# Elementwise work of a token mixer taken off GpSimd and given to VectorE and ScalarE

## The chip, the cores and the metric

The kernel runs on one core of a Trainium2 chip. The metric is device microseconds from the start to the end of one execution; lower is better. A core has five engines that each run their own instructions in a fixed order and wait for one another by semaphores: TensorE (PE in the profile; its weight loads are the row PEld), VectorE (DVE), ScalarE (ACT), GpSimd (POOL) and SyncE (SP), which here only issues DMA transfers.

## The reference

One decoder layer on 1024 tokens of width 1024, all in float32: a half-step feed-forward network (FFN) with layer norm, a token mixer with layer norm, a second half-step FFN with layer norm, and a gated embedding. The change touches the mixer alone. Cut to what it touches:

```
z = x1 @ w_in                                   # 1024 x 1024 -> 3872 columns
# four retention pairs of heads (u), chunks of 128 tokens
q, k = rotary(q), rotary(k) / 8                 # t*cos + swapped(t)*sin
ret  = (q k^T * decay) v + (q * qdecay) @ state
ret_out = silu(g) * (groupnorm(ret) * gain + bias)
# four RWKV-7 pairs of heads (u): one step for each token
state = state * w_t - (state @ kk_t) b_t + v_t k_t ;  y_t = state @ r_t
k  = k * (1 + (a - 1) * k_a)
rw_out  = (groupnorm(y) * gain + bias + bonus * v) * gate
x2 = layer_norm(alpha * x1 + [ret_out, rw_out] @ w_out)
```

The token-by-token recurrence is computed in chunks of 128 tokens. The log decays are summed along a chunk (`cs`), and each chunk's factors are `exp(cs - middle)` and `exp(middle - cs)`, where the middle is `cs` at token 64 of the chunk.

## The kernel before

The mixer takes about 700 to 1550 us of the span. Features lie on the 128 partitions and tokens along the free axis. The RWKV part has 8 units: four head pairs `u`, each with two halves `h` of 512 tokens, so names such as `w2_1` or `r1_1` are unit `u_h` of RWKV (w) or of retention (r). The loop over steps `s` in `mixer` does, at step `s`, for three units at different stages: `rw_operands` of unit `s+1` (products with the chunk factors, and a triangular inverse by 31 pairs of small VectorE instructions, `itw` L1040 and `ixw` L1042, in `substitution`), `doublings` and `rw_chunks` of unit `s` (the chain over the four chunks through the state `wst`), `rw_inputs` of unit `s+2` (shift, low-rank projections, decays, normalised keys), and `retention` of unit `s`.

The products `z` with the weights `w_in` are filler for TensorE: 28 tiles (`z_tile`) at a low priority, 48 products of 128x512 each. As float32 is split into a high and a low part (`split`: ScalarE casts the high part, L47; another engine subtracts it to make the low part, L48), each product is three matmuls, L61 to L63, and L63 needs the low part `lo_win`. The split of a tile's weights can't begin before the matmuls on the tile before have read the same buffers. When the z tiles are done, the products with `w_out` (`wopo`, weights and rows split into `mw`) are the filler.

Nobody writes an order by hand: a list scheduler orders each engine's instructions at build time, by dependencies, the priorities in the code, and its own estimates of durations. On the chip the order is fixed, so an instruction that waits holds up all that stand behind it on its engine.

GpSimd does in the mixer, before the change: the low parts of `w_in` (54 of 56 instructions) and half of those for `w_out`; in `rw_inputs` the subtraction of the middle (`ccw` L953), two small instructions for the state's factor `few`, and the product of the keys `wkw` L982; in `rw_operands` `arw` L1013 and `kpw` L1015; in `rw_chunks` the scaled state `sfw` L1136 and two products of the output, `wow` L1155 and L1156; in `retention` four rotary instructions (L842, L844), the decay of q (`zqr` L867) and the output's product (`ror` L902). The bonus product on TensorE, `bnpw` L987, needs `rkw` L985 on VectorE, which needs `wkw` L982 on GpSimd, which comes after `kkw` L981 on VectorE. The transpose `ktpr` needs `zkr` L844.

## Time and profile before

| | us |
|---|---|
| median of 3 runs | 2352.06 (2345.69 to 2354.2) |
| profiled execution | 2348.16 |
| its span in the profile | 2346.4 |
| TensorE busy | 2247.1 (96%) |
| VectorE busy | 1631.9 (70%) |
| ScalarE busy | 833.8 (36%) |
| GpSimd busy | 755.3 (32%) |

The profile is one execution. 1.8 us of its time lie outside the span. Busy time of an engine counts its instructions from start to end; on TensorE matmuls overlap and their ends are modelled, so the times between starts say more than the busy share. The granted clock is that of TensorE, as a share of 2.4 GHz.

### The profile page before, as it was taken

The page shows a single profiled execution, that of the slowest core. Times are in us where ns is not written, and L with a number is a line of the kernel's source. Part 1 is how long each engine was busy: PE and PEld are TensorE (multiplying, and loading weights), DVE is VectorE, ACT ScalarE, POOL GpSimd, SP SyncE. Part 2 cuts the span into 40 slices and gives each one's busy share as a digit, 9 for nine tenths or more (in the row PEclk, how much of TensorE's full clock was granted, in tenths as well). Part 3 has the DMA queues.
Part 4 walks back from the last instruction along what each step waited for, and adds up shares of the span by engine and source line. Part 5 has one row for each costly group of instructions (what it writes and reads, how often), then busy time and mean ns, then how long its engine had stood idle before and what let it go on. Part 6 is the DMA issues. An engine that isn't in the chain of part 4 may idle for free.

```text
span 2346.4 us, 31303 instructions
## 1 busy us (share of the span) xinstructions
PE 2247.1 (96%) x11009; PEld 1801.9 (77%) x11009; DVE 1631.9 (70%) x2643; ACT 833.8 (36%) x1418; POOL 755.3 (32%) x614
## 2 busy tenths in 40 slices
PE   7999999999999999999999999998999999999999
PEld 5888888788786667777677777766888888788787
DVE  7776867765782378576774777689676767966862
ACT  4322232344652523232332323263323232445550
POOL 4346464300102323334433433225555553000220
PEclk9999999999999999799999999999999999999999
DMA  4345555497335443133333363323464644974321
GB/s 145 122 152 177 173 190 166 162 334 237 89 121 180 145 130 96 58 117 113 96 102 118 94 187 116 99 90 104 153 195 155 202 144 148 354 256 149 111 77 41
DMA packets 288963, 345.97 MB, mean 147 GB/s; under 512 B 35715, under 2 KB 162150, under 8 KB 288806
## 3 DMA queue, kind: packets, MB, share of 16 engines
q1 hardware_dynamic: 284224, 331.34, 44.2%
q0 software_dynamic: 3328, 12.06, 1.3%
q8 instruction: 87, 1.43, 0.3%
q10 hardware_dynamic: 1254, 0.58, 0.1%
q14 instruction: 70, 0.57, 0.1%
HBM read 237.47 MB, written 106.43 MB: 147 GB/s over the span
## 4 chain that ended last, share of the span: by engine, by line
PE 77%; DVE 14%; issue 3%; DMA 3%; POOL 2%; ACT 1%; SPq 0%; ACTq 0%; DVEq 0%; POOLq 0%
PE f2m L62 5%; PE f2m L63 5%; PE f2m L61 5%; PE f1m L61 5%; PE f1m L62 5%; PE f1m L63 5%; PE z L63 3%; PE z L61 3%; PE z L62 3%; DVE ixw L1042 2%; DVE itw L1040 2%; PE scpw L1102 2%; PE f1qa L61 1%; PE f1qa L62 1%; PE f1qa L63 1%
## 5 line engine op out<-in xcount | busy, mean ns | idle before, releaser
L61 PE MATMUL z<-x1Th,hi_win 128*128 128x512 f32 x448 | 188.2, 420 | 4.6 <-ACT hi_win L47 4.6
L63 PE MATMUL z<-x1Th,lo_win 128*128 128x512 f32 x448 | 188.2, 420 | 4.5 <-POOL lo_win L48 3.4
L62 PE MATMUL z<-x1Tl,hi_win 128*128 128x512 f32 x448 | 187.9, 419 | 0.0
L1040 DVE TENSOR_TENSOR itw<-iltw,ixw 32x31 f32<-32x31 f32 (+15 forms) x248 | 114.1, 460 | 24.3 <-DMA iltw<-scrw 10.7
L1042 DVE TENSOR_TENSOR ixw<-ixw,itw 32x31 f32<-32x31 f32 (+15 forms) x248 | 110.4, 445 | 4.5
L48 POOL TENSOR_TENSOR lo_win<-raw_win,hi_win 128x512 fp32r<-128x512 f32 x54 | 75.9, 1407 | 116.5 <-ACT hi_win L47 102.3
L61 PEld LDWEIGHTS z<-x1Th,hi_win 128*128 128x128 f32 x448 | 86.9, 194 | 28.5 <-ACT hi_win L47 5.7
L63 PEld LDWEIGHTS z<-x1Th,lo_win 128*128 128x128 f32 x448 | 86.4, 193 | 26.7 <-POOL lo_win L48 5.8
L62 PEld LDWEIGHTS z<-x1Tl,hi_win 128*128 128x128 f32 x448 | 86.4, 193 | 19.9 <-issue 2.1
L149 POOL TENSOR_TENSOR f2tb<-f2tb,f2tb 128x512 f32<-128x512 f32 x44 | 71.5, 1626 | 80.4 <-DMA f2tb<-in_ffn_w_down 74.4
L149 POOL TENSOR_TENSOR f1tb<-f1tb,f1tb 128x512 f32<-128x512 f32 x44 | 69.7, 1583 | 70.4 <-DMA f1tb<-in_ffn_w_down 66.1
L48 DVE TENSOR_TENSOR f1hl<-f1s,f1hh 128x512 fp32r<-128x512 f32 x63 | 45.5, 723 | 62.4 <-ACT f1hh L47 62.4
L48 DVE TENSOR_TENSOR f2hl<-f2s,f2hh 128x512 fp32r<-128x512 f32 x63 | 44.9, 713 | 44.4 <-ACT f2hh L47 44.4
L47 ACT CAST f1hh<-f1s 128x512 fp32r<-128x512 f32 x63 | 39.2, 622 | 92.2 <-PE f1qa L62 38.6
L47 ACT CAST f2hh<-f2s 128x512 fp32r<-128x512 f32 x63 | 39.2, 622 | 89.7 <-PE f2qb L62 35.1
L1136 POOL TENSOR_SCALAR sfw<-wst,few 64x64 f32<-64x64 f32 x48 | 30.1, 628 | 125.8 <-DVE wst L1137 77.0
L1110 DVE COPY_PREDICATED scz<-mask,scpw 128x384 f32<-128x384 uint8 x64 | 36.7, 584 | 46.6 <-PE scpw L1105 38.8
L108 DVE TENSOR_TENSOR f2S<-f2w 128x512 f32<-128x512 f32 x22 | 20.6, 939 | 65.2 <-DMA f2w<-in_ffn_w_gu 62.4
L62 PE MATMUL f2qa<-f2vl,f2hh 128*128 128x512 f32 x164 | 64.1, 391 | 0.7 <-DVE f2vl L48 0.7
L63 PE MATMUL f2qa<-f2vh,f2hl 128*128 128x512 f32 x164 | 64.0, 390 | 0.3 <-DVE f2hl L48 0.3
L62 PE MATMUL f1qa<-f1vl,f1hh 128*128 128x512 f32 x164 | 63.9, 389 | 0.0
L63 PE MATMUL f1qa<-f1vh,f1hl 128*128 128x512 f32 x164 | 63.8, 389 | 0.0
(786 smaller groups left out, 7117.5 us busy)
## 6 DMA issues: line engine op xcount, KB each, us to landing
f1w<-in_ffn_w_gu SPq DMA_DIRECT2D x44, 512.0 KB
f2w<-in_ffn_w_gu SPq DMA_DIRECT2D x44, 512.0 KB
f1s<-hd SPq DMA_DIRECT2D x63, 256.0 KB
f2s<-hd SPq DMA_DIRECT2D x63, 256.0 KB
zs<-zs SPq DMA_DIRECT2D x56, 256.0 KB
raw_win<-in_w_in SPq DMA_DIRECT2D x54, 256.0 KB
f1tb<-in_ffn_w_down SPq DMA_DIRECT2D x44, 256.0 KB
wt<-f1tb SPq DMA_DIRECT2D x44, 256.0 KB
```

The source lines that it names most:

```text
L47: self.last_split = self.nc.scalar.copy(hi, src).ins
L48: (eng or self.nc.vector).tensor_tensor(out=lo, in0=src, in1=hi, op=ALU.subtract)
L61: mm(ps, a[0], b[0], start=first, stop=False)
L62: mm(ps, a[0], b[1], start=False, stop=False)
L63: mm(ps, a[1], b[0], start=False, stop=last)
L108: sub = lambda o, a, b, op=ALU.subtract: V.tensor_tensor(out=o, in0=a, in1=b, op=op)
L149: nc.gpsimd.tensor_tensor(out=t, in0=a, in1=b, op=ALU.subtract)
L1040: nc.vector.tensor_tensor(out=t, in0=lt[:, j, j + 1:].unsqueeze(2).broadcast_to([B, n, c]), in1=x[:, j:j + 1, 0:c].broadcast_to([B, n, c]) ...
L1042: nc.vector.tensor_tensor(out=x[:, j + 1:, 0:c], in0=x[:, j + 1:, 0:c], in1=t, op=ALU.add)
L1102: nc.tensor.matmul(ps[e][:, 0:2 * P], kp[rr, cs], ar[rr, c].rearrange("p a t -> p (a t)"), start=True, stop=True)
L1110: nc.vector.copy_predicated(z, self.mask, ps[e][:, 0:3 * P].rearrange("p (a t) -> p a t", a=3))
L1136: nc.gpsimd.tensor_scalar(out=sf[rr], in0=st[rr, rr], scalar1=fe[rr, c:c + 1], scalar2=None, op0=ALU.mult)
```

## The change

All arithmetic that GpSimd did in the mixer goes to VectorE, but for the scaled state `sfw`, which goes to ScalarE. GpSimd keeps its memsets and DMA issues. The subtraction of the middle is dropped: ScalarE's exponentials take the middle as a bias for each partition instead, so that each chunk needs its own two instructions (8 for a unit where there were 2), and VectorE makes the four negated middles (`mid`). The output of an RWKV unit, before one ScalarE and two GpSimd instructions, becomes two VectorE instructions with a scalar for each partition.

```diff
# retention (both q and k)
-            nc.gpsimd.tensor_tensor(out=b, in0=b, in1=sin, op=ALU.mult)
+            nc.vector.tensor_tensor(out=b, in0=b, in1=sin, op=ALU.mult)
             nc.vector.tensor_tensor(out=a, in0=a, in1=cos, op=ALU.mult)
-            nc.gpsimd.tensor_tensor(out=a, in0=a, in1=b, op=ALU.add)
+            nc.vector.tensor_tensor(out=a, in0=a, in1=b, op=ALU.add)
-        nc.gpsimd.tensor_tensor(out=qd, in0=qd, in1=qdec.broadcast_to([P, 4, P]), op=ALU.mult)
+        nc.vector.tensor_tensor(out=qd, in0=qd, in1=qdec.broadcast_to([P, 4, P]), op=ALU.mult)
-        nc.gpsimd.tensor_tensor(out=t, in0=t, in1=th, op=ALU.mult)
+        nc.vector.tensor_tensor(out=t, in0=t, in1=th, op=ALU.mult)
# rw_inputs
-        cc = tmp("cc", 4 * (P + 1)).rearrange("p (c t) -> p c t", c=4)
-        nc.gpsimd.tensor_tensor(out=cc, in0=cs, in1=cs[:, :, 64:65].broadcast_to([P, 4, P + 1]), op=ALU.subtract)
+        mid = T("mid", [4])
+        nc.vector.tensor_scalar(out=mid, in0=cs[:, :, 64], scalar1=-1.0, scalar2=None, op0=ALU.mult)
-        nc.scalar.activation(w.eP, cc, AF.Exp)
-        nc.scalar.activation(w.eM, cc[:, :, 1:], AF.Exp, scale=-1.0)
+        for c in range(4):
+            nc.scalar.activation(w.eP[:, c], cs[:, c], AF.Exp, bias=mid[:, c:c + 1])
+            nc.scalar.activation(w.eM[:, c], cs[:, c, 1:], AF.Exp, bias=cs[:, c, 64:65], scale=-1.0)
-        nc.gpsimd.tensor_copy(w.fe, w.eP[:, :, P])
-        nc.gpsimd.tensor_tensor(out=w.fe[:, 0:3], in0=w.fe[:, 0:3], in1=w.fm[:, 1:4], op=ALU.mult)
+        nc.vector.tensor_copy(w.fe, w.eP[:, :, P])
+        nc.vector.tensor_tensor(out=w.fe[:, 0:3], in0=w.fe[:, 0:3], in1=w.fm[:, 1:4], op=ALU.mult)
-        nc.gpsimd.tensor_tensor(out=k, in0=k, in1=kf, op=ALU.mult)
+        nc.vector.tensor_tensor(out=k, in0=k, in1=kf, op=ALU.mult)
# rw_operands
-        nc.gpsimd.tensor_tensor(out=w.ar[:, :, 1], in0=c4(w.r), in1=w.eP[:, :, 1:], op=ALU.mult)
+        nc.vector.tensor_tensor(out=w.ar[:, :, 1], in0=c4(w.r), in1=w.eP[:, :, 1:], op=ALU.mult)
-        nc.gpsimd.tensor_tensor(out=c4(w.kp), in0=c4(w.k), in1=w.eM, op=ALU.mult)
+        nc.vector.tensor_tensor(out=c4(w.kp), in0=c4(w.k), in1=w.eM, op=ALU.mult)
# rw_chunks
-                        nc.gpsimd.tensor_scalar(out=sf[rr], in0=st[rr, rr], scalar1=fe[rr, c:c + 1], scalar2=None, op0=ALU.mult)
+                        nc.scalar.activation(sf[rr], st[rr, rr], AF.Copy, scale=fe[rr, c:c + 1])
-        nc.scalar.activation(t, yt, AF.Identity, bias=self.pc("rw_gn_b", u), scale=self.pc("rw_gn_g", u))
-        nc.gpsimd.tensor_tensor(out=t, in0=t, in1=bv, op=ALU.add)
-        nc.gpsimd.tensor_tensor(out=t, in0=t, in1=gt, op=ALU.mult)
+        nc.vector.scalar_tensor_tensor(out=t, in0=yt, scalar=self.pc("rw_gn_g", u), in1=bv, op0=ALU.mult, op1=ALU.add)
+        nc.vector.scalar_tensor_tensor(out=t, in0=t, scalar=self.pc("rw_gn_b", u), in1=gt, op0=ALU.add, op1=ALU.mult)
# w_out_operand, and the call of z_tile in mixer
-            self.split(*parts, raw, self.nc.gpsimd if i else self.nc.vector)
+            self.split(*parts, raw)
-                    self.z_tile(x1T, c0, zs[idx[c0]], *((nc.scalar, nc.vector) if early else (nc.sync, nc.gpsimd)))
+                    self.z_tile(x1T, c0, zs[idx[c0]], nc.scalar if early else nc.sync, nc.vector)
```

The order of instructions moves with it. The first place is the stage at which unit w1_1 ends its last chunk, unit w2_1 makes its inputs and retention r1_1 begins. On GpSimd stood there, before (a name's first number is the unit, the last one only counts tiles):

```order
L842 TENSOR_TENSOR zqsr1_1_10087<-zqsr1_1_10087,sinr1_1_10078 128x512
L844 TENSOR_TENSOR zqr1_1_10085<-zqr1_1_10085,zqsr1_1_10087 128x512
L982 TENSOR_TENSOR wkw2_1_10005<-wkw2_1_10005,kfw2_1_10047 128x512
L1015 TENSOR_TENSOR kpw2_1_10579<-wkw2_1_10005,eMw2_1_10039 128x512
L842 TENSOR_TENSOR zksr1_1_10097<-zksr1_1_10097,sinr1_1_10078 128x512
L48 TENSOR_TENSOR lo_win2432_0_9495<-raw_win2432_0_9492,hi_win2432_0_9494 128x512
L844 TENSOR_TENSOR zkr1_1_10095<-zkr1_1_10095,zksr1_1_10097 128x512
L1155 TENSOR_TENSOR wow1_1_9993<-wow1_1_9993,bvw1_1_9989 128x512
L1156 TENSOR_TENSOR wow1_1_9993<-wow1_1_9993,gtw1_1_9991 128x512
```

Now these stand on VectorE, each between two instructions of the triangular inverse of unit w2_0 (`itw`, `ixw`). From the output of w1_1 to the rotated k of r1_1:

```order
L1155 SCALAR_TENSOR_TENSOR wow1_1_10020<-ytpw1_1_10011,pcol_1830,bvw1_1_10016 128x512
L1041 TENSOR_TENSOR itw2_014_9724<-iltw2_0_9674,ixw2_0_9679 32x255
L1156 SCALAR_TENSOR_TENSOR wow1_1_10020<-wow1_1_10020,pcol_1830,gtw1_1_10018 128x512
L1043 TENSOR_TENSOR ixw2_0_9679<-ixw2_0_9679,itw2_014_9724 32x17x15
L986 SCALAR_TENSOR_TENSOR rkw2_1_10103<-wrw2_1_10037,pcol_1830,wkw2_1_10031 128x512
L1041 TENSOR_TENSOR itw2_015_9727<-iltw2_0_9674,ixw2_0_9679 32x256
L842 TENSOR_TENSOR zksr1_1_10129<-zksr1_1_10129,sinr1_1_10110 128x512
L1043 TENSOR_TENSOR ixw2_0_9679<-ixw2_0_9679,itw2_015_9727 32x16x16
L989 TENSOR_TENSOR rkw2_1_10103<-wvw2_1_10043,bnpw2_1_10105 128x512
L1041 TENSOR_TENSOR itw2_016_9730<-iltw2_0_9674,ixw2_0_9679 32x255
L844 TENSOR_TENSOR zkr1_1_10127<-zkr1_1_10127,zksr1_1_10129 128x512
```

Two rows ahead of these stands `wkw2_1`, and 16 rows behind them the next low part of a filler tile, `lo_win2432_0`: what two engines did side by side is one row, and `rkw` and `zkr` come behind the output of the unit before.

The second place is TensorE at the same stage. Before:

```order
L63 MATMUL z2944_1_9464<-x1Th_3697,lo_win2944_0_9427 128x512
L61 MATMUL z2944_1_9464<-x1Th_3697,hi_win2944_1_9432 128x512
L987 MATMUL bnpw2_1_10073<-rkw2_1_10071,ones_6335 128x512
L62 MATMUL z2944_1_9464<-x1Tl4_3702,hi_win2944_1_9432 128x512
L819 MATMUL vtpr1_1_10108<-ident_58,zvr1_1_10105 128x128 x4
L63 MATMUL z2944_1_9464<-x1Th_3697,lo_win2944_1_9433 128x512
L819 MATMUL ktpr1_1_10115<-ident_58,zkr1_1_10095 128x128 x4
L862 MATMUL rspr1_10_10122<-zqr1_1_10085,zkr1_1_10095 128x128 x3
L61 MATMUL z2944_1_9464<-x1Th_3697,hi_win2944_1_9432 128x512
L819 MATMUL ytpw1_1_9984<-ident_58,gnyw1_1_9974 128x128 x4
```

Now:

```order
L61 MATMUL z2432_1_9559<-x1Th_3697,hi_win2432_0_9521 128x512
L62 MATMUL z2432_1_9559<-x1Tl0_3698,hi_win2432_0_9521 128x512
L819 MATMUL ytpw1_1_10011<-ident_58,gnyw1_1_10001 128x128 x4
L988 MATMUL bnpw2_1_10105<-rkw2_1_10103,ones_6335 128x512
L819 MATMUL vtpr1_1_10140<-ident_58,zvr1_1_10137 128x128 x4
L819 MATMUL ktpr1_1_10147<-ident_58,zkr1_1_10127 128x128 x4
L862 MATMUL rspr1_10_10154<-zqr1_1_10117,zkr1_1_10127 128x128 x4
L862 MATMUL rspr1_11_10155<-zqr1_1_10117,zkr1_1_10127 128x128 x4
L872 MATMUL kvpr1_1_10167<-vtr1_1_10139,kdr1_1_10146 128x128 x4
L879 MATMUL yor1_1_10168<-rst1_6360,zqr1_1_10117 128x128
L882 MATMUL yor1_1_10168<-vtr1_1_10139,rscr1_1_10153 128x64 x2
L63 MATMUL z2432_0_9531<-x1Th_3697,lo_win2432_0_9522 128x512
```

The tile z2944 is finished ahead of this stage (29 filler matmuls stand between the transposes `rnpw2_1` and `ytpw1_1`, where 14 stood between `rnpw2_1` and `bnpw2_1`), and between `ytpw1_1` and `lo_win2432_0` no filler is left.

The third place is ScalarE in unit w1_1's second chunk, beside the decays of unit w2_1. Before:

```order
L1120 COPY rhsw1_11_9897<-chw1_11_9893 128x128
L1125 COPY saw1_11_9901<-chw1_11_9893 128x128
L961 ACTIVATE fmw2_1_10042<-csw2_1_10030 128x4
L956 ACTIVATE ePw2_1_10038<-ccw2_1_10036 128x516
L957 ACTIVATE eMw2_1_10039<-ccw2_1_10036 128x512
L944 ACTIVATE athw2_1_10027<-apw2_1_10023,pder_1851 128x512
L1146 COPY yrw1_1_9850<-chw1_11_9893 128x128
```

Now:

```order
L1121 COPY rhsw1_11_9924<-chw1_11_9920 128x128
L1126 COPY saw1_11_9928<-chw1_11_9920 128x128
L958 ACTIVATE eMw2_1_10065<-csw2_1_10056 128x128 x3
L957 ACTIVATE ePw2_1_10064<-csw2_1_10056,midw2_1_10062 128x129
L1137 ACTIVATE sfw1_120_9964<-wst0_6362,few1_1_8473 64x64
L1137 ACTIVATE sfw1_121_9967<-wst0_6362,few1_1_8473 64x64
L957 ACTIVATE ePw2_1_10064<-csw2_1_10056,midw2_1_10062 128x129 x2
L944 ACTIVATE athw2_1_10053<-apw2_1_10049,pder_1851 128x512
```

The exponentials are in pieces, and the two scaled states of the next chunk stand among them.

## Rows read from the trace of the kernel before

**Rows 1.** Busy time of each engine (share of the span) and instructions

```profile
PE 2247.1 (96%) x11009; PEld 1801.9 (77%) x11009; DVE 1631.9 (70%) x2643; ACT 833.8 (36%) x1418; POOL 755.3 (32%) x614
```

**Rows 2.** Stretches: length, busy PE PEld DVE ACT POOL, granted clock, DMA

```profile
700.00:1550.00 850.00, 801.49 (x4598) 617.55 (x4598) 549.60 (x1160) 265.95 (x491) 280.24 (x292) 0.95 0.38 117
820.00:830.00 10.00, 7.19 (x30) 5.03 (x29) 8.18 (x17) 0.62 (x1) 4.47 (x3) 0.73 0.22 48
1140.00:1150.00 10.00, 7.23 (x35) 5.30 (x34) 8.92 (x11) 2.45 (x6) 8.90 (x6) 0.95 0.16 53
1150.00:1160.00 10.00, 7.33 (x25) 5.42 (x25) 9.48 (x17) 1.18 (x2) 4.66 (x5) 0.54 0.46 136
```

**Rows 3.** TensorE's waits in 700 to 1560: us, times, longest us

```profile
PE bnpw L987 <- DVE rkw L985: 10.3, 5, 2.8
PE ktpr L819 <- POOL zkr L844: 4.7, 2, 2.7
PE chw L1140 <- DVE wst L1137: 4.3, 6, 1.3
PE z L63 <- POOL lo_win L48: 3.4, 3, 2.0
```

**Rows 4.** Chain that ended last, 700 to 800: start, us, what

```profile
778.55 1.75 POOL wkw L982
780.32 1.86 DVE rkw L985
```

**Rows 5.** Instructions in order of time, 1136 to 1160: start, us, [idle before]

```profile
1140.75 0.27 ACT L1146 COPY yrw<-chw 128x128 f32<-128x128 f32 x1 [1.42 <-PE chw L1145]
...
1144.74 1.88 POOL L982 TENSOR_TENSOR wkw<-wkw,kfw 128x512 f32<-128x512 f32 x1 [0.95 <-DVE kkw L981]
...
1145.41 1.46 DVE L1040 TENSOR_TENSOR itw<-iltw,ixw 32x231 f32<-32x231 f32 x1
...
1147.68 1.10 PE L987 MATMUL bnpw<-rkw,ones 128*128 128x512 f32 x2 [2.77 <-DVE rkw L985]
...
1152.88 1.11 PE L819 MATMUL ktpr<-ident,zkr 128*128 128x128 f32 x4 [2.67 <-POOL zkr L844]
...
1155.81 0.67 DVE L1002 TENSOR_TENSOR bbw<-bbw,eMw 128x512 f32<-128x512 f32 x1
...
1156.41 0.41 DVE L1040 TENSOR_TENSOR itw<-iltw,ixw 32x255 f32<-32x255 f32 x1
...
1156.75 0.67 DVE L852 TENSOR_TENSOR kdr<-ktpr,kdec 128x512 f32<-128x512 f32 x1
```

**Rows 6.** Groups on GpSimd and VectorE in the mixer: busy us, mean ns

```profile
L48 POOL TENSOR_TENSOR lo_win<-raw_win,hi_win 128x512 fp32r<-128x512 f32 x54 | 75.9, 1407 | 116.5 <-ACT hi_win L47 102.3
L953 POOL TENSOR_TENSOR ccw<-csw 128x516 f32<-128x516 f32 x8 | 8.5, 1056 | 39.6 <-DVE csw L950 31.9 <-issue 4.7 <-PE chw L1123 3.0
L999 DVE TENSOR_TENSOR arw<-kkw,ePw 128x512 f32<-128x512 f32 x8 | 5.4, 678 | 0.1
L805 DVE TENSOR_SCALAR gstr<-gstr 128x8 f32<-128x8 f32 x8 | 1.3, 163 | 0.1
L1040 DVE TENSOR_TENSOR itw<-iltw,ixw 32x31 f32<-32x31 f32 (+15 forms) x248 | 114.1, 460 | 24.3 <-DMA iltw<-scrw 10.7
L1042 DVE TENSOR_TENSOR ixw<-ixw,itw 32x31 f32<-32x31 f32 (+15 forms) x248 | 110.4, 445 | 4.5
```

**Rows 7.** One line of VectorE: shortest, median and longest, in ns

```profile
L1040 DVE TENSOR_TENSOR itw<-iltw,ixw x248: 169/364/1493, 823.4 to 1416.3; 32x31 f32<-32x31 f32 x8, 32x87 f32<-32x87 f32 x8, 32x135 f32<-32x135 f32 x8, 32x175 f32<-32x175 f32 x8
```

**Rows 8.** Groups on ScalarE in the mixer: busy us, mean ns

```profile
L760 ACT ACTIVATE smkw<-wzkw,pder 128x512 f32<-128x512 f32 x8 | 5.8, 724 | 3.9 <-DMA wzkw<-zs 3.4 <-DVE ld L779 0.5
L956 ACT ACTIVATE ePw<-ccw 128x516 f32<-128x516 f32 x8 | 5.1, 633 | 3.3 <-POOL ccw L953 3.2
L961 ACT ACTIVATE fmw<-csw 128x4 f32<-128x4 f32 x8 | 1.7, 208 | 4.9 <-DVE csw L950 4.9
```

**Rows 9.** Instructions in order of time near the mixer's end

```profile
1531.34 0.50 PE L62 MATMUL wopo<-mw 128*128 128x512 f32 x1 [1.08 <-POOL mw L48]
```

## The prediction

> **What bounds the kernel now.** I read the busy times first: TensorE 96%, VectorE 70%, GpSimd 32% [rows 1]. So only what TensorE loses counts. Next the mixer's stretch, 700 to 1550 us: TensorE is busy for 801.5 of 850 us, so no more than 48.5 us of idle time is there to win. Its granted clock is .95 [rows 2]; if the rest is spent at the lower of the two levels (1.2 instead of 2.4 GHz), that is .05 / .5 × 850 = 85 us at half clock, worth at most 42 us. VectorE fills 65% of the mixer, but not evenly: from 1140 to 1160 it is busy 18.4 of 20 us, and TensorE idles 5.4 us there [rows 2]. Third, TensorE's waits: the four largest that end on VectorE or GpSimd sum to 22.7 us, led by `bnpw` on `rkw` with 10.3 us in five [rows 3]. The chain of waits shows why: at 778.55 GpSimd's `wkw` takes 1.75 us, and `rkw` behind it 1.86 us [rows 4]. Last, the timeline shows what such a wait does later: `bnpw` starts at 1147.68 after 2.77 us of idling, `ktpr` after 2.67 us, and the next 10 us run at a granted clock of .54 [rows 2, 5].
>
> **VectorE's added work.** It takes 158 instructions of 128x512: 54 `lo_win`, 16 `mw`, 32 rotary, 8 for q's decay, 8 retention outputs, 16 for `arw` and `kpw`, 8 `wkw` and 16 for the outputs of the RWKV units. The nearest row is `arw`, .678 us [rows 6]: 158 × .678 = 107 us. The 24 small ones (`mid`, `few`) go by `gstr`, .163 us [rows 6]: 4 us. Together 111 us. GpSimd needed 1.41 us for a `lo_win` [rows 6], so a step that TensorE waits for is shorter now if VectorE is free for it.
>
> **What VectorE gets back.** The steps of the inverse are the gauge. Step t works on t(32 − t) columns (31, 87, 135, 175 for t = 1, 3, 5, 7), 176 in the mean. The shortest of `itw` takes .169 us [rows 7], which I take as the time for 31 columns undisturbed; one of 255 took .41 us [rows 5]. On the line between them 176 columns take .325 us. The groups show .460 and .445 [rows 6]: 248 × (.135 + .120) = 63 us longer than that. The longest, 1.46 us for 231 columns, lies beside a `wkw` on GpSimd that runs from 1144.74 to 1146.62 [rows 5]. A lower bound is mean less median of `itw`, 248 × (.460 − .364) = 24 us; I take 63, since the line is through undisturbed instructions of known size. VectorE in the mixer: 549.6 − 63 + 111 = 598 us, 70% of the stretch, from 65%. Lengthenings of its other instructions come on top, so 598 is an upper estimate of my own sum.
>
> The Trainium skill has a rule on this (SBUF — State Buffer, section "SBUF: two separate sides"): VectorE and GpSimd share a pair of ports as an exclusive lock, and a VectorE instruction with two inputs from SBUF and a GpSimd one that reads SBUF shut each other out for a whole instruction. The trace agrees with it: 1.46 us beside GpSimd's `wkw`, .41 us without. By the rule all lengthening goes, that of other two-input instructions too, and the 111 us would be paid back nearly in full; by the rows 63 of 111 are. Its own result is the first rival.
>
> **ScalarE.** Two exponentials of 516 and 512 columns become eight of 129 and 128. With a fixed part as in `fm` (.208 us for 4 columns) and a slope from `smk` against it, (724 − 208) / 508 = 1.02 ns a column, one would take .335 us; `eP`, without a pointer, has a slope of .83, and a start with one is dearer by 724 − 633 = .09 us, so I take .406. Eight are 3.2 us where 1.25 stood, +2 us for a unit [rows 8]. Against that `ccw` with 1.06 us becomes `mid` with .16 [rows 6]: +1.1 us on the way to the products of a unit. Between bounds of 0 (covered by filler) and 1.1 for each of 8 units I charge the first two units alone, where little is ahead: +2.2. Forty-eight `sfw` at about .35 us (bounds .21 and .72, rows of the same group) add 17 us; ScalarE rises from 266 to some 293 of 850 us less the eight affine instructions dropped, and stays hidden. `sfw` needs only the state of the chunk before, as the addend of the next, so I price its place among the exponentials at 0; were it late, `wst` would pay, whose waits are 4.3 us now [rows 3].
>
> **The sum**, against the profiled execution's own 2348.2 us, which is 0.2% under the median of 2352.06.
> - First two units, near 780 and 821 us: two `bnpw` waits, 2.1 us each (10.3 / 5). `wkw` goes from 1.75 to .68 and `rkw` from 1.86 to some .74 [rows 4], 2.2 us off the path, more than the 2.1 waited; I count 1.8 each: −3.6. The 10 us from 820 have a clock of .73 [rows 2], so 5.4 of them are at half; for this and the like stretch behind 780 I give back 3.
> - `lo_win`: three waits, 3.4 us [rows 3]. .68 us instead of 1.41, but in VectorE's row behind other work: −2 (bounds −3.4 and 0).
> - The last products: one wait of 1.08 us for `mw` [rows 9]: −1.
> - `wst` waits and VectorE's steps that are no longer stretched, on the chain over chunks: −4 for the waits (4.3 at most [rows 3]) and −4 for bursts like that of 18.4 in 20 us, which hold up TensorE and get shorter; bounds 0 and, with the 5.4 us idled in such a burst in place of the 4, −10.
> - Exponentials: +2.2.
> - The two late stages (w2_1 beside r1_1, and w3_1 beside r2_1): here the orders decide. Now 14 instructions of 512 columns stand on VectorE from `wow` to `lo_win2432_0` (`wow` twice, `rkw`, `zks`, `rkw`, `zkr`, `arw`, `bbw` twice, `kdr`, two for the scores, q's decay, `lo_win`), with 13 inverse steps between. Starts lie .60 us apart behind a product of 512 columns and .34 behind a step [rows 5]: 14 × .60 + 13 × .34 = 12.8 us, and TensorE has no filler in this time, only its eight groups from `ytpw` to `yor`. `bnpw` and `ktpr` took 1.10 and 1.11 us at half clock [rows 5], so about .5 at full, and next groups start before those ends: I take 3 us for the eight, an estimate. It idles some 10 us. Ahead of that the 29 filler matmuls hide VectorE's row from `yrw` to `ytpw` (7 products, 7 steps: 6.6 us), as 14 of them took from 1140.75 to the start of the wait, 1147.68 − 2.77, at most .30 us each. Before, TensorE idled 5.4 us in this stage. So +4.5 for each of the two, +9. The inverse gets some four steps further meanwhile, which the following stage need not wait for, and I give 3 back: +6.
>
> −3.6 − 3 − 2 − 1 − 4 − 4 + 2.2 + 6 = −9.4: **2339 us**. Each saving has its cover in TensorE's filler: without filler ahead, as in the late stages, VectorE's .60 us for each instruction lies on the path in full.
>
> **Rivals.** *Contention was the brake.* What for: the line above gives 63 us for two lines alone, and every two-input instruction may have been stretched. Then VectorE is no fuller than before, and all the waits of the four rows go (22.7), the tail's 1.1, and the half clock behind them: a stretch at .54 is 9.2 of 10 us at half, at a busy share of .73 worth 3.4, twice, and 1.9 at 820; less 2.2 for the exponentials: 2348 − 30 = **2318**. Against it: the late stages' row of 12.8 us is counted with undisturbed times already.
>
> *The waits only change their name.* `bnpw`, `ktpr` and `lo_win` wait for VectorE instead of GpSimd, since VectorE has one row where two ran side by side. The early savings (the first, second and third items with the tail: 3.6 + 3 + 2 + 1 = 9.6) and the late stages at +9 cancel: **2348**. For it: TensorE's 801.5 busy us in the mixer stay, and the largest wait, `bnpw`, ends on a VectorE instruction already [rows 3]. Against it: at 780 us VectorE has room, as what is late there is GpSimd's own 1.75 us [rows 4].
>
> *VectorE becomes the bound* (slower). The mechanism is the one row of VectorE in the stages where a unit's inverse, the next unit's inputs and a retention fall together. If that costs 4.5 us not in two stages but in each of six units that overlap so, because `lo_win` stands behind up to 13 instructions and the filler runs out, it is +27 and +2.2, less the 9.6: 2348.2 + 19.6 = **2368**. It is decided from 3.8 us a unit: 6 × 3.8 + 2.2 − 9.6 = 15.4, which is the bound for slower. For it: 18.4 of 20 us busy already. Against it: in the mean 30% of VectorE stays free.
>
> **Chances.** About 0.5% (11.8 us) is what a measurement of this kernel can tell: faster is below 2340, slower above 2364. Forecast .42, with its own range 2331 to 2347 (the bounds of `lo_win` and `wst`, and the late stages at 0 to +12), .29 of it below 2340 and .13 above; contention .15, renamed waits .20, VectorE the bound .23. So faster .44, same .33, slower .23. The range reaches to the centre of the slower case and past that of the fast one: 2312 to 2368.
>
> **What the profile of the changed kernel would show.** Right: `itw` and `ixw` at a mean near .33 us with none at 1.4; VectorE near 600 us in the mixer; `bnpw` waiting under .5 us in the first two units; ten us of idling on TensorE between `ytpw` and the first `lo_win` of the two late stages; `sfw` on ScalarE without a wait of `wst` on it. Wrong: VectorE at 550 or less (contention was the brake); TensorE waiting for `lo_win` or `bnpw` on VectorE in the early units too (renamed, or the bound); idling of 4 us or more in units other than the two late ones; or a granted clock in the mixer below .95, since idling that I counted once would then be paid for twice.

## The result, and the profile after

The changed kernel is slower: 2381.93 us (median, 2375.82 to 2391.68) against 2348.88 us of the kernel before on the same chips, a ratio of 1.0143 with a 95% interval of 1.0101 to 1.0186. The prediction was 2339 us, with 2368 us as its upper end. The profiled execution took 2380.59 us, with a span of 2378.4 us, 32 more than before.

The first part of the changed kernel's page, busy times, answers to [rows 1]:

```profile
PE 2274.3 (96%) x11009; PEld 1817.0 (76%) x11009; DVE 1643.3 (69%) x2825; ACT 861.5 (36%) x1510; POOL 494.0 (21%) x384
```

GpSimd lost 261 us of work, and VectorE gained only 11, though it has 182 instructions more. TensorE, which does the same 11009 matmuls, is 27 us longer busy. So by these means no engine but TensorE is full, and there the same matmuls took longer. The groups of the changed kernel say that the work itself cost what was foreseen, or less (columns as in [rows 6, 8]):

```profile
L1043 DVE TENSOR_TENSOR ixw<-ixw,itw 32x31 f32<-32x31 f32 (+15 forms) x248 | 80.6, 325 | 3.3
L1041 DVE TENSOR_TENSOR itw<-iltw,ixw 32x31 f32<-32x31 f32 (+15 forms) x248 | 80.0, 323 | 2.8
L48 DVE TENSOR_TENSOR lo_win<-raw_win,hi_win 128x512 fp32r<-128x512 f32 x56 | 38.0, 681 | 55.8 <-ACT hi_win L47 53.5 <-DMA zkr<-zs 2.1
L1137 ACT ACTIVATE sfw<-wst,few 64x64 f32<-64x64 f32 x48 | 16.6, 345 | 41.6 <-DVE wst L1138 23.4 <-DVE wst L1099 11.5 <-DVE wst L1134 6.3
L957 ACT ACTIVATE ePw<-csw,midw 128x129 f32<-128x129 f32 x32 | 11.4, 397 | 1.3 <-DVE midw L953 1.3
```

The inverse's steps are at .325 and .323 us, `lo_win` takes .681, `sfw` .345 and a piece of the exponentials .397. The loss is in when things happen. Stretches of the changed kernel, columns as in [rows 2]:

```profile
700.00:1550.00 850.00, 796.35 (x4442) 606.82 (x4441) 536.63 (x1282) 280.05 (x564) 18.95 (x58) 0.93 0.37 113
1056.00:1078.00 22.00, 14.23 (x69) 11.53 (x68) 16.91 (x48) 6.53 (x16) 0.00 (x0) 0.65 0.16 48
1096.00:1106.00 10.00, 10.00 (x47) 5.59 (x48) 0.16 (x1) 1.00 (x2) 0.00 (x0) 1.00 0.16 56
1178.00:1194.00 16.00, 11.34 (x44) 8.87 (x43) 14.50 (x31) 0.59 (x2) 0.00 (x0) 0.62 0.24 78
```

Two kinds of stretch stand out. From 1056 to 1078 and from 1178 to 1194 TensorE has little to do and a mean granted clock of .65 and .62. From 1096 to 1106 it is busy all the time at full clock and yet gets only 47 matmuls done, two thirds of them small ones of 64x64. TensorE's largest waits, as in [rows 3]:

```profile
PE z L63 <- DVE lo_win L48: 8.1, 4, 4.7
PE bnpw L988 <- DVE rkw L986: 6.6, 3, 3.2
PE ytpw L819 <- DVE gnyw L812: 6.0, 1, 6.0
PE z L61 <- ACT hi_win L47: 4.0, 1, 4.0
...
PE chw L1141 <- DVE wst L1138: 3.3, 6, 1.0
```

The early waits for `rkw`, at 780 and 821 us, are gone; the filler's wait for `lo_win` has more than doubled. That wait shows only a part of what is late. The timeline of the changed kernel has the high parts of one tile, and where their low parts come:

```profile
1033.44 0.62 ACT L47 CAST hi_win<-raw_win 128x512 fp32r<-128x512 f32 x1 [0.40 <-PE z L62]
...
1050.16 0.62 ACT L47 CAST hi_win<-raw_win 128x512 fp32r<-128x512 f32 x1 [2.20 <-PE z L62]
...
1077.01 0.67 DVE L48 TENSOR_TENSOR lo_win<-raw_win,hi_win 128x512 fp32r<-128x512 f32 x1
...
1077.74 0.80 PE L63 MATMUL z<-x1Th,lo_win 128*128 128x512 f32 x1 [4.68 <-DVE lo_win L48]
...
1077.83 0.63 DVE L48 TENSOR_TENSOR lo_win<-raw_win,hi_win 128x512 fp32r<-128x512 f32 x1
```

The two high parts are ready at 1034.1 and 1050.8, and VectorE makes the low parts at 1077.0 and 1077.8: 43 and 27 us later. From start of `lo_win` less end of `hi_win`, over all 56, the mean is .9 us before and 4.6 us now. Four stretches without filler, from 1056, 1177, 1260 and 1368 us and 63 us in all, end within a microsecond behind such a late `lo_win`; 41 of the 123 us at half clock (table below) lie in them. The kernel before has stretches without filler too, of 8 to 23 us, but none of them ends behind a late low part.

The second kind of stretch, on TensorE from 1095.9:

```profile
1095.90 0.32 PE L1062 MATMUL i1w<-Xd,M 64*64 64x64 f32 x2
1096.15 0.50 PE L61 MATMUL z<-x1Th,hi_win 128*128 128x512 f32 x1
1096.59 0.33 PE L1062 MATMUL i1w<-Xd,M 64*64 64x64 f32 x2
1096.84 0.49 PE L62 MATMUL z<-x1Tl,hi_win 128*128 128x512 f32 x1
1097.27 0.33 PE L1062 MATMUL i1w<-Xd,M 64*64 64x64 f32 x2
```

The 64x64 products of the block inverse (`i1w` to `i4w`) alternate one by one with filler: one product, which leaves two records, and a filler matmul take .69 us (1095.90 to 1096.59). In TensorE's row before there are 64 changes between these products and other matmuls, now 188, most of the new ones in units w1_1 and w2_1. A third view puts both together: the last filler matmul with a low part of `w_in` starts at 1392.5 before and at 1434.1 now (the matmuls that read the low parts, with their first and last start):

```profile
L63 PE MATMUL z<-x1Th,lo_win x448: 388/397/794, 719.8 to 1392.5; 128*128 128x512 f32 x150
```

```profile
L63 PE MATMUL z<-x1Th,lo_win x448: 387/396/796, 718.7 to 1434.1; 128*128 128x512 f32 x150
```

An account of the 32 us of span, from the matmuls and clock records of the two profiled executions: the time of matmuls that began at half clock goes from 98 to 123 us, which at full clock would be half, so +12; 124 changes at .17 us (measured below) are an estimate of +21; the span less TensorE's busy time goes from 99 to 104, +5. That is 38; the other matmuls together took 6 us less, which I have not traced further.

### The profile page after: what moved, and what is told of

Its sections match the earlier page's. It is cut to its first block, busy times and chain, and to the rows that moved or that the text cites. A ratio compares the mean times of both kernels' runs of the same rounds, so it can differ in the third digit from the quotient of the medians.

```text
span 2378.4 us, 31216 instructions
## 1 busy us (share of the span) xinstructions
PE 2274.3 (96%) x11009; PEld 1817.0 (76%) x11009; DVE 1643.3 (69%) x2825; ACT 861.5 (36%) x1510; POOL 494.0 (21%) x384
## 5 line engine op out<-in xcount | busy, mean ns | idle before, releaser
L1043 DVE TENSOR_TENSOR ixw<-ixw,itw 32x31 f32<-32x31 f32 (+15 forms) x248 | 80.6, 325 | 3.3
L1041 DVE TENSOR_TENSOR itw<-iltw,ixw 32x31 f32<-32x31 f32 (+15 forms) x248 | 80.0, 323 | 2.8
L1035 POOL MEMSET ixw<- 32x1024 f32 x8 | 7.6, 946 | 354.4 <-DMA scsw<-ixw 328.8
L48 DVE TENSOR_TENSOR lo_win<-raw_win,hi_win 128x512 fp32r<-128x512 f32 x56 | 38.0, 681 | 55.8 <-ACT hi_win L47 53.5
L149 POOL TENSOR_TENSOR f1tb<-f1tb,f1tb 128x512 f32<-128x512 f32 x44 | 64.7, 1471 | 31.0 <-DMA f1tb<-in_ffn_w_down 24.5
L661 ACT COPY zs<-z 128x512 f32<-128x512 f32 x56 | 32.7, 584 | 104.8 <-PE z L63 99.8
L47 ACT CAST hi_win<-raw_win 128x512 fp32r<-128x512 f32 x56 | 34.5, 619 | 89.6 <-PE z L62 82.8
```

The costliest lines, as they stand in the source:

```text
L47: self.last_split = self.nc.scalar.copy(hi, src).ins
L48: (eng or self.nc.vector).tensor_tensor(out=lo, in0=src, in1=hi, op=ALU.subtract)
L149: nc.gpsimd.tensor_tensor(out=t, in0=a, in1=b, op=ALU.subtract)
L661: nc.scalar.copy(zs, ps)
L1035: nc.gpsimd.memset(x, 0.0)
L1041: nc.vector.tensor_tensor(out=t, in0=lt[:, j, j + 1:].unsqueeze(2).broadcast_to([B, n, c]), in1=x[:, j:j + 1, 0:c].broadcast_to([B, n, c]) ...
```

## The experiments

Ratios are to the kernel before on the same chip, where its median was 2349 to 2352 us; changes are those in TensorE's row between `i1w` to `i4w` and other matmuls. The half clock (clock records that begin between 690 and 1620 us) and the last column are of the one profiled execution, which can lie up to 23 us from the median (filler_later: 2402.81, 18 above it).

The two columns between are means over a kernel's executions, from the span and the mean granted clock that each one lists. Span × (1 − clock) is the most that the lower level can have cost, since time in which TensorE has nothing to do costs nothing at either level; span × clock is the rest, called full-clock time here. Full-clock time varies by 1 to 4 us (standard deviation) among the executions of one kernel, where the span varies by 1 to 12: where the spread is large, most of it is the clock. For the changed kernel it is 12 us more at full clock and up to 20 more lost to the clock.

| kernel | us | ratio, 95% | changes | span × clock | span × (1 − clock) | half clock, us | mean us from high to low part |
|---|---|---|---|---|---|---|---|
| before | 2348.88 | 1 | 64 | 2292 | 57 | 92 | .9 |
| changed | 2381.93 | 1.0143 (1.0101 to 1.0186) | 188 | 2304 | 77 | 123 | 4.6 |
| blocks_first | 2366.12 | 1.0063 (1.0040 to 1.0086) | 54 | 2286 | 78 | 137 | 4.9 |
| filler_later | 2384.89 | 1.0149 (1.0097 to 1.0201) | 46 | 2290 | 95 | 212 | 3.9 |
| win_back_on_gpsimd | 2364.48 | 1.0042 (1.0017 to 1.0067) | 62 | 2283 | 78 | 126 | .9 |
| win_alone_on_vector | 2371.10 | 1.0083 (1.0057 to 1.0108) | 46 | 2288 | 79 | 147 | 3.5 |
| low_parts_first | 2337.31 | .9938 (.9920 to .9955) | 54 | 2264 | 71 | 126 | .8 |
| win_alone_first | 2360.77 | 1.0047 (1.0015 to 1.0079) | 84 | 2293 | 67 | 130 | 1.2 |
| retention_alone | 2334.54 | .9920 (.9888 to .9951) | 46 | 2284 | 48 | 89 | 1.0 |
| low_first_w_out_earlier | 2312.27 | .9836 (.9798 to .9875) | 72 | 2261 | 49 | 102 | .8 |
| before_w_out_earlier | 2354.82 | 1.0033 (1.0003 to 1.0063) | 78 | 2295 | 59 | 99 | 1.1 |
| low_first_gpsimd_aside | 2429.95 | 1.0328 (1.0279 to 1.0377) | 74 | 2306 | 121 | 212 | 1.7 |
| low_first_gpsimd_busy | 2482.26 | 1.0584 (1.0530 to 1.0638) | 52 | 2339 | 134 | 218 | 1.3 |

**The block products in runs.** Theory A was that the alternation costs the time, theory B that VectorE's one row does.

```diff
+        with self.tc.high_priority(offset=100):
             for r, i in diagonal:
                 nc.tensor.matmul(ps[r, 64 * i:64 * i + 64], w.M1[r, i, r], self.Xd[r, i, r], ...)
```

and the same around `i2` to `i5`.

> The changed kernel, with the products of 64x64 of the block inverse (i1 to i5) at a higher priority, so that TensorE's row has them in runs: it changes between them and other matmuls 54 times, where the changed kernel does so 188 times and the kernel before 64 times. All of VectorE's added work stays. Theory A (the alternation of 64x64 products with filler on TensorE costs about .18 us for each change, from .69 us for a pair and a filler matmul at 1096 us against .32 us apart): 134 fewer changes, -25 us, about 2357. Theory B (VectorE's one row is the bound, TensorE starves at half clock): no change beyond 5 us, 2377 to 2387. Both, with half clock as the rest: 2357 to 2365, and the granted clock in the mixer stays near .93.

Measured: 2366 us, 16 less than the changed kernel, just above the 2357 to 2365 of both theories together, and still 15 more than before. `i1w` runs together again:

```profile
1089.24 1.14 PE L1063 MATMUL i1w<-Xd,M 64*64 64x64 f32 x30
```

Alternation is a cause and holds about half of the loss. Low parts are as late as ever (4.9 us in the mean), and the half clock even rose to 137 us, which at half its time takes back 7 of the 25 us hoped for. Over all executions the full-clock time is 18 us less than the changed kernel's and the loss to the clock 1 more.

**The filler at a lower priority**, which alters only rows:

```diff
-FILLER = -300
+FILLER = -400
```

> The changed kernel with the priority offset of the filler at -400 in place of -300, which changes only the order of rows: 46 changes between 64x64 products and other matmuls, no alternation one by one. Theory A: 142 fewer changes, -26 us, about 2356. Theory B: the same instructions on VectorE, the filler no earlier: 2375 to 2390.

Measured: 2385 us, no gain, although the alternation is gone. Theory A alone falls here: low parts are late (3.9 us). Over all executions the full-clock time is 14 us less than the changed kernel's, and the loss to the clock 18 more, which takes it all back (the 212 us at half clock are of the slowest execution). The numbers of theory B fit, but VectorE's work is the same as in the run above that gained 16 us; what differs is when TensorE has filler.

**The low parts back, and alone.** One part undone in the changed kernel, and the same part done alone in the kernel before:

```diff
-self.z_tile(x1T, c0, zs[idx[c0]], nc.scalar if early else nc.sync, nc.vector)
+self.z_tile(x1T, c0, zs[idx[c0]], *((nc.scalar, nc.vector) if early else (nc.sync, nc.gpsimd)))
```

> The changed kernel with the low parts of w_in on GpSimd again, all else as changed. TensorE's row changes between 64x64 products and others 62 times. Theory A: 126 fewer changes, -23 us, about 2359, and the waits for lo_win (8.1 us) fall to about 3, -5: 2354. Theory B: VectorE loses 54 x .68 = 37 us of work and the filler no longer stands in its row, so the half clock goes too: 2340 to 2350, and the granted clock rises to .95.

> The kernel before with the low parts of w_in alone moved to VectorE. TensorE's row has 46 changes, fewer than the 64 of before. Theory A: no loss from alternation, 18 fewer changes, -3 us: 2340 to 2350. Theory B: the filler's splits stand in VectorE's row behind other work as in the changed kernel, and a good part of the loss is there already: 2355 to 2370, with TensorE's waits for lo_win at 5 us or more and a clock below .95.

Measured: 2364 and 2371 us. Moving the low parts is the harmful part: alone it costs some 20 us (.83%) with fewer changes than before, so not by alternation, and undoing it takes back 17. Alone, the whole loss is in the clock: 4 us less at full clock, 22 more lost. Theory A is refuted as the only cause, since win_alone_on_vector has 46 changes. Neither run comes to the time before, and the expectation of B for the first (2340 to 2350) is missed too; for the second B's time holds, and its waits for `lo_win`, 4.8 us, come just short of 5. The first one's trace has a stretch at 1358 to 1424 us in which the filler with `w_in` is used up and that with `w_out` has hardly begun, at a clock of .56:

```profile
1358.00:1424.00 66.00, 49.02 (x277) 43.01 (x275) 31.86 (x81) 12.43 (x31) 0.00 (x0) 0.56 0.35 113
```

**The low parts first.** This led to theory C: the low parts of the filler have the filler's low priority, and on VectorE, which is full of work of higher priority, their row is far back; on GpSimd nothing stood in front of them. The test alters one priority and no work:

```diff
-        self.split(hi, lo, raw, eng)
+        self.last_split = self.nc.scalar.copy(hi, raw).ins
+        with self.tc.high_priority(offset=600):
+            (eng or self.nc.vector).tensor_tensor(out=lo, in0=raw, in1=hi, op=ALU.subtract)
```

> The changed kernel, with the low parts of w_in on VectorE at a higher priority (offset 600), so that they stand right behind their high parts in VectorE's row; no work changes. In the changed kernel four of them end 14 to 26 us after their high part, and TensorE runs 11 to 21 us without filler each time, mostly at half clock. In this kernel's row the alternation of 64x64 products and filler is gone as well (54 changes instead of 188). Theory C (late low parts are the cause of both the half clock and the alternation): no filler matmul waits more than 2 us for a low part, half clock in the mixer falls from 123 to about 95 us, and the time to 2345 to 2358. Rival D (the added work on VectorE itself is the cost): only the alternation goes, 2362 to 2370, as with the products in runs.

Measured: 2337 us, 45 us less than the changed kernel with the same instructions (the expectation's 14 to 26 us fit the second low parts of the changed kernel's tiles; the first are up to 43 us late), and faster than the kernel before (.9938, .9920 to .9955). The filler with `w_in` ends 92 us earlier than in the changed kernel:

```profile
L65 PE MATMUL z<-x1Th,lo_win x448: 388/395/797, 718.6 to 1341.9; 128*128 128x512 f32 x150
```

It waits for low parts for 1.4 us in all (8.1), and the alternation is gone without anything done about it. One number of the expectation failed: the half clock stays at 126 us. It has only moved, to the end of the filler:

```profile
700.00:1550.00 850.00, 808.06 (x4626) 632.86 (x4624) 578.00 (x1364) 293.43 (x592) 22.77 (x65) 0.93 0.38 120
1342.00:1402.00 60.00, 46.08 (x263) 38.95 (x262) 28.60 (x70) 12.14 (x30) 0.00 (x0) 0.54 0.40 130
```

Between 1342 and 1402 the clock is .54. So the gain is 40 us of full-clock time and at most 6 of the clock. By the probe's price below, 134 changes are 23 of it, and the span less TensorE's busy time, 104 to 88 us, is 16. The raised priority also lets the scheduler place the other rows anew, and the 45 us hold that too.

**The same priority with the low parts alone**, on the kernel before:

> The kernel before with only the low parts of w_in moved to VectorE, at the same raised priority. Moved without it they cost 18 to 20 us (2371). TensorE's row has 84 changes between 64x64 products and others (64 before), worth +4. Theory C: about 2351 + 4 = 2350 to 2358. Rival D: 37 us more on VectorE cost the same wherever they stand, 2366 to 2375.

Measured: 2361 us, 10 less than without the priority, 10 more than before. Both theories' ranges are missed, each by a little. The low parts are no longer late (1.2 us); 84 changes would be worth +3.5 by the probe. But the full-clock time is that of the kernel before, 2293 against 2292 us, and the loss to the clock is 10 us more: the low parts are in time, and TensorE still loses its clock. What leaves it without filler there stays open.

**Retention alone** (the rotary instructions, q's decay and the output's product, 48 in all, as in the diff):

> The kernel before with retention's arithmetic alone moved to VectorE (48 instructions, some 33 us); the low parts stay on GpSimd, 46 changes on TensorE's row (64 before, -3). Theory C: the filler's splits are not touched, 2345 to 2355, with less waiting for zkr in the two late stages (4.7 us before). Rival D: a share of the loss by work added, 33 of 111 us, some +10: 2360.

Measured: 2335 us, .9920 (.9888 to .9951), better than theory C gave it. VectorE got 33 us more to do and the kernel became faster. Its inverse steps are at .416 and .411 us, where [rows 6] has .460 and .445. Work added on VectorE thus does not cost by itself, as theory D had it; GpSimd is relieved by the same instructions here, and the rows have 18 changes fewer. The gain is 8 us at full clock and at most 9 of the clock.

**What a change between the products costs.** Behind the last matmul of the kernel before, with `blocks` two products of 64x64 on the two halves of the rows, and `full` two with weights of 128x128 and 64 columns of output:

```diff
+            for f in (blocks, full):
+                for _ in range(64):
+                    f()
+                    fill()
+                for _ in range(64):
+                    f()
+                for _ in range(64):
+                    fill()
```

> The kernel before with a block of matmuls behind its last one, whose results nobody reads: 64 pairs of 64x64 products (one on the lower, one on the upper half of the rows) each followed by one 128x512 matmul, then the same 128 and 64 apart; then the same with products that use all 128 rows and 64 columns. Theory A: a pair and a 128x512 matmul take .69 us alternated and .32 us apart, .37 us for two changes. If it is the change between half the rows and all of them, the second kind shows no difference (under .05 us); if it is any small matmul between long ones, both do.

TensorE's timeline of it, the end of the first kind and of the second:

```profile
2398.25 0.33 PE L1492 MATMUL prp<-prw 64*64 64x64 f32 x4
2398.51 0.50 PE L1488 MATMUL prp<-prr 128*128 128x512 f32 x1
2398.94 0.33 PE L1492 MATMUL prp<-prw 64*64 64x64 f32 x4
...
2399.64 7.68 PE L1492 MATMUL prp<-prw 64*64 64x64 f32 x256
2407.25 14.81 PE L1488 MATMUL prp<-prr 128*128 128x512 f32 x64
2421.89 0.55 PE L1496 MATMUL prp<-prw 128*128 128x64 f32 x4
...
2463.84 0.55 PE L1496 MATMUL prp<-prw 128*128 128x64 f32 x4
2464.21 0.48 PE L1488 MATMUL prp<-prr 128*128 128x512 f32 x1
2464.52 0.55 PE L1496 MATMUL prp<-prw 128*128 128x64 f32 x4
...
2465.20 28.70 PE L1496 MATMUL prp<-prw 128*128 128x64 f32 x256
2493.70 14.80 PE L1488 MATMUL prp<-prr 128*128 128x512 f32 x64
```

Alternated, a 64x64 pair and a long matmul take .69 us (2398.25 to 2398.94). Apart, 64 pairs start over 7.61 us (2399.64 to 2407.25), .119 each, and the long ones, 64 in 14.64 us up to the next block's start at 2421.89, are .229: .348 together. So alternating costs .345 us, .17 for each change. With products on the whole array (128*128 in the rows) it is .68 alternated and .445 + .229 = .674 apart: nothing. It is the change between 64x64 and the whole array, not the small matmul; whether the rows or the columns count is not told apart. In the kernel one product, not a pair, stands between two filler matmuls: .69 us against .06 + .229, which makes .20 a change, an estimate. So the expectation's .69 for a pair in the kernel was misread, and the 21 us of the account may be 25.

**GpSimd loaded again.** Does the freed contention count? Twice the kernel with the low parts first got dead work on GpSimd; first, behind each split:

```diff
+        for _ in range(3):
+            self.nc.gpsimd.tensor_tensor(out=d, in0=raw, in1=hi, op=ALU.subtract)
```

> The kernel with the low parts first, to which GpSimd does 168 subtractions of 128x512 in the mixer (three for each split of w_in, on its raw and high parts, into a tile that nobody reads): about the load that it had before the change, some 1.3 us each. Everything else is as it was. If the lengthening of VectorE's instructions beside GpSimd is a brake of its own: itw and ixw go from .32 back to .40 or more, VectorE's busy time in the mixer rises by 40 us or more, and the time to 2350 to 2365 (of which a little can be raw parts held longer). If it is hidden behind TensorE: the lengthening shows, and the time stays at 2335 to 2345.

Measured: 2482 us. This holds the filler's buffers for some 4.7 us a split, so it can't price contention; a second run keeps off them:

```diff
+        for _ in range(20):
+            nc.gpsimd.tensor_tensor(out=self.dum, in0=self.dum, in1=w.fm[:, 0:1].broadcast_to([P, HALF]), op=ALU.mult)
```

> The kernel with the low parts first, and on GpSimd 20 products of 128x512 behind the decays of each unit (160 in all, some 1.3 us each or 26 us for a unit) on a tile of its own that nobody reads, so that no buffer of the kernel is held by them. TensorE's row changes 74 times between 64x64 products and others (54), worth +3.5. Were the 145 us of the last run the buffers held by GpSimd's reads, the contention itself is small: 2340 to 2350. Is the lengthening beside GpSimd a brake: itw and ixw at .38 or more, VectorE 30 us busier in the mixer, 2350 to 2370.

Measured: 2430 us, 93 more than without, far over either range. Its groups:

```profile
L966 POOL TENSOR_TENSOR dum<-dum,fmw 128x512 f32<-128x512 f32 x160 | 191.3, 1195 | 134.1 <-ACT fmw L964 122.5
L1045 DVE TENSOR_TENSOR itw<-iltw,ixw 32x31 f32<-32x31 f32 (+15 forms) x248 | 108.6, 438 | 29.6 <-DMA iltw<-scrw 21.0 <-POOL ixw L1040 5.4
L1047 DVE TENSOR_TENSOR ixw<-ixw,itw 32x31 f32<-32x31 f32 (+15 forms) x248 | 105.2, 424 | 3.1
```

191 us of GpSimd's work, bound to nothing but `fm`, make the inverse's 496 steps 53 us longer (213.8 against 160.7) and put 212 us of the mixer at half clock; of the 93 us, 42 are full-clock time and at most 50 the clock. That contention brakes this kernel is shown in kind; its price isn't, since GpSimd's memsets, for which the inverse waits 5.4 us here, now stand behind the dead work too, and the rows have 20 changes more.

**A faster version.** The stretch of .54 at the end of the filler with `w_in` pointed to the filler behind it:

```diff
-            rows = {5: [((4, 0), (0, 1))], 6: ...
+            rows = {4: [((4, 0), (0, 1))], 6: ...
-                    if s == 5:
+                    if s == 4:
```

> The kernel with the low parts first, and the first group of products with w_out one step earlier in the code. With the low parts first the filler of w_in ends at 1342 us, and up to 1402 TensorE runs 59 us with almost no filler, 54 of them at half clock. If the filler that follows comes in earlier, half clock in the mixer falls from 126 to 90 us or less, and the time to 2320 to 2330; TensorE's row has 72 changes between 64x64 products and others (54), +3. If what the group waits for (the rows' buffers, freed by the last product with w_in) decides, nothing moves: 2335 to 2342.

> The kernel before with the first group of products with w_out one step earlier in the code, as in the fastest version, and nothing else. It has only 23 us without filler at the end of the products with w_in (1393 to 1416), 11 of them at half clock, where the version with the low parts first had 59. TensorE's row has 78 changes (64), +2.5. If the gain of the fastest version belongs to the faster filler of the changed arithmetic: 2340 to 2355 here. If it is as much a gain of its own: 2320 to 2335.

Measured: 2312 us (.9836, .9798 to .9875) with the low parts first, and 2355 (1.0033) on the kernel before. The stretch itself, in the faster version:

```profile
1342.00:1402.00 60.00, 44.30 (x272) 34.62 (x270) 37.76 (x81) 11.85 (x20) 0.00 (x0) 0.86 0.57 181
```

Its clock is .86, where it was .54, and of the 25 us gained over low_parts_first up to 22 are the clock. Of these two kernels the step is worth something only where the filler with `w_in` ends early (1342 us, against 1392 before), which the changed arithmetic brings about once its low parts are in time.

## Why the prediction was wrong

**The step that failed** is the item on `lo_win`: ".68 us instead of 1.41, but in VectorE's row behind other work: −2 (bounds −3.4 and 0)". It priced the instruction and its three waits, not its place. The place decided: 43 and 27 us late at the worst, 63 us without filler in four stretches, and, in the rows, the alternation of 64x64 products with the filler that piled up. In low_parts_first the priority that sets this place is worth 45 us, the alternation that went with it included.

**What was in no term** is the alternation. The prediction read TensorE's row at the late stage and not where the block inverse stands, although the counts 64 and 188 could be had from the order alone. By the probe's .17 us, 124 changes are 21 us; taking out 134 gave 16 us, 18 at full clock. Why late low parts lead the scheduler to alternate is only argued from the two going away together.

**The clock** stands in the sum with 3 us given back behind the early waits; it cost up to 20 us instead. The sign for it that the prediction named came true: .93 in the mixer, below .95. Another sign came without its meaning: VectorE is at 536.6 us, "550 or less", but the stretch up to 1550 holds 1282 of its instructions, where 1160 and 182 more were to be expected; the changed mixer ends later.

**The late stages**: 10 us of idling between `ytpw` and `lo_win` were forecast for two stages. The changed kernel's timeline at the first of them answers to [rows 5]:

```profile
1181.51 1.66 PE L988 MATMUL bnpw<-rkw,ones 128*128 128x512 f32 x2 [3.20 <-DVE rkw L986]
...
1184.88 1.11 PE L819 MATMUL ktpr<-ident,zkr 128*128 128x128 f32 x4 [0.85 <-DVE zkr L844]
```

`bnpw` waits 3.20 us and `ktpr` .85; from 1178 to 1194 TensorE idles 4.7 of 16 us, at a mean clock of .62 over the stretch. The length of the stretch, 16 us against 12.8, was nearly right, its split wrong: I took 3 us at full clock for TensorE's groups, which were busy for 11.3 us. And four stretches without filler ended behind a late low part, not two.

**What held.** The early `bnpw` waits vanished; unit w0_0's inverse starts at 818.8 instead of 823.4, 4.5 us earlier (3.6 and a share of 3 forecast). The inverse's steps came to .325 and .323 (.325 forecast from the line through the shortest and the 255-column step). `lo_win` took .681 (.678), the exponentials .397 (.406), `sfw` .345 (.35), and none of TensorE's waits above ends on the last two. The inverse's 496 steps got back 64 us (63 forecast), and the other VectorE lines that the mixer had before some 13 more, in the trace: 77 of the 111 us came back, not 63 and not nearly all. The chain's wait for `wst` fell from 4.3 to 3.3 us, where 4 were forecast. With another priority the same arithmetic gives 2337 us, near the forecast of 2339, but by other terms: 28 us less than before at full clock and up to 14 more lost to the clock. That agreement is luck.

**The rivals.** "VectorE becomes the bound" had the mechanism, `lo_win` behind up to 13 instructions and filler that runs out, and the sign; at 2368 it lacked the alternation. But its name is wrong: VectorE is busy for 536.6 of 850 us only, though for 14.5 of 16 in the stretch at 1178, and one priority undoes it. "Contention was the brake" is supported in kind, not in price, by the dead work on GpSimd and by retention_alone; in the changed kernel the two losses outweigh what it gives.

On the alternation the Trainium skill has a rule (TensorEngine Tiling (Array Packing), section "Tiling Modes", "Key Properties"): a change of the tiling mode drains TensorE. The probe agrees, with .17 us for a change here and nothing where both kinds of product use the whole array.

## What to carry to other kernels

Work moved to another engine takes its priority along: low-priority work that feeds TensorE's filler was prompt here on an idle engine and late on a full one (.9 and 4.6 us in the mean), so look at how far it stands behind its producer in the new row, not only at its duration. Read TensorE's whole row for changed neighbours, and count changes between products of 64x64 and matmuls on the whole array: each cost .17 to .20 us here. Multiply each execution's span by its mean clock before a difference of 10 us is explained: what is left of it is work and waiting, and the rest is the clock, which here was low where TensorE was short of filler. When a change of arithmetic loses, try it again with one priority set right before it is dropped; here that turned 1.4% slower into .6% faster, and a further step, worth nothing before, then gave another 1%.

## What the runs showed of the hardware that was not expected

- A pair of 64x64 products and a 128x512 matmul take .69 us alternated and .348 apart; with products on the whole array it is .68 and .674.
- 191 us of GpSimd's elementwise work beside VectorE made a kernel of 2337 us 93 us longer, partly by the lengthening of VectorE's steps (.32 to .43 us in the mean), partly by what stood behind it on GpSimd.
- The 64 executions of the kernel before have spans of 2336 to 2365 us; times their mean granted clock (.969 to .982) they differ by a standard deviation of 3 us only.
